# Where a transformer block's kernel copies and sums a set of combined weights

## The chip, the cores and the metric

The kernel runs on one core of a Trainium2 chip. The metric is the device time of one execution in microseconds; lower is better. The core has a matrix engine (TensorE, PE in the profile), a vector engine (VectorE, DVE), a scalar engine (ScalarE, ACT), GpSimd (POOL) and SyncE (SP). SP computes nothing here: it issues most of the transfers between the off-chip memory and the on-chip memory. ACT and POOL issue transfers too. Each engine works through its own list of instructions in order and waits on semaphores where an instruction needs another engine's or a transfer's result.

## The reference

One layer of a diffusion block, in fp32, for 1024 latent tokens and 256 context tokens of width 1024:

```python
h_x = _modulate(x, g_pre_mix[l], sh1, sc1)           # RMSNorm, gain, scale, shift
u_x, q_x, k_x, v_x = _project(h_x, w_in[l])
attn_x = _neighbourhood_attention(q_x, k_x, v_x, k_c, v_c, rpb[l])
mix_x = jnp.concatenate([_pool_mixer(u_x, pool_w[l], pool_scale[l]), attn_x], axis=-1) @ w_out[l]
x = x + gt1 * _rmsnorm(mix_x, g_post_mix[l])
y_x = _sq_relu_mlp(_modulate(x, g_pre_mlp[l], sh2, sc2), w_mlp_in[l], w_mlp_out[l])
x = x + gt2 * _rmsnorm(y_x, g_post_mlp[l])
```

The neighbourhood attention has 8 heads and adds a learned bias `rpb`, masked to a window, to the scores of the local keys. The MLP is relu(h @ w1) squared, times w2, with a hidden width of 4096.

## The kernel before

Every large product is done from operands split into a high and a low part (three matrix products for one), and most of the large products are one level of a seven-product scheme (Strassen's, in Winograd's form) over 2 x 2 blocks. That scheme needs sums and differences of the blocks of the weights. For the MLP's second product (`w2`), three such combinations are made ahead of time in off-chip memory, each in eight pages of 512 KB (g = 0 to 7): `t3` (block 1,1 plus block 0,1), `t1` (block 0,1 of `w2` plus block 0,0) and `t2` (block 1,1 plus `t1`). For each page there is one copy, `block_copied`, a transfer from `w2` to the page issued by SP (line 1329), and one sum, `block_summed`, a transfer that adds onto the page, issued by POOL (`add_to`, line 211). The 24 copies go in the order t3, t1, t2, and so do the 24 sums. The pages are first read in the second MLP product, from 815 us on (`t2`), 817 us on (`t3`) and 880 us on (`t1`).

The stages, in order of time: the normalised tokens and the pooling mixer's input, the context's keys, the values, then the *key products* (lines 1147 to 1176: 24 steps of twelve matrix products each, `step` 0 to 23, giving keys and queries), then *attention* (`for i in range(N)`, line 1447: 32 rounds, one for each of four pairs of heads and eight column tiles of 128 queries), the output projection, and the MLP: the *first product* goes over 16 pairs of hidden blocks (`block_pair(p)`, p = 0 to 15), the second over eight groups.

What sets the order: `with in_order(...)` ties every instruction of the listed engines to the one before it on the same engine in the block, as written; outside of it a planner orders each engine's list by its own estimate of when things are ready. The key products are in such a block for PE, POOL, ACT, DVE and SP (`pooling`), attention in another for PE, ACT, DVE and SP (`projected`) and one for POOL; pairs 1 to 14 of the MLP's first product are tied on PE and POOL.

Things to follow:
- `use(step)` splits the weights that were loaded four places ago and loads more (`load`, line 201) into a ring of four buffers, the tag `raw`. `mask_page()` at step 14 loads the mask (line 1057). `tables(0)` at step 20 loads the bias rows `U0w` (line 1069) into the same ring and has POOL subtract them from the mask into two pages `tab` (line 1077). `pool_mixed` at steps 21 and 22 splits the pooling mixer's output into pages `mix` of the same ring (lines 171 and 177).
- `key_parts` and `query_parts` split the keys and queries into high and low parts, `kP` and `qP`, which `scores(i)` reads (line 1223). `biased(i, e)` adds the tables to the scores (line 1243).
- In attention, round i issues two copies for i < 4 and one for 4 <= i < 16, after four ahead of the rounds, and `SUMS` lists the rounds that issue a sum. Five more sums go behind the output projection's rows.
- In the MLP's first product `summed_behind(c22)` (line 2024) lets ACT copy one column of a pair's result and POOL copy that again, so that the sum which POOL issues next comes no sooner than that result. Before the change, pairs 3 to 11 do so, once each.
- From pair 10 on, `ahead()` also sums up the row of the second gate, `accb`: POOL clears a page and loads a bias row (lines 238 and 239), and DVE adds eight weighted rows `wmb` to it (line 246).

Of the kernel before, what the change touches and what calls it, by code (L numbers as in the profile page):

```python
# [11 lines left out]
F32 = mybir.dt.float32  # L12
# [6 lines left out]
P = 128  # L19
# [84 lines left out]
def hybrid_block(ctx, tc, x, ctx_in, w_mod, mod_pages, w_u, b_mod, gp1, gp2, w_in, pool_w, rpb, w_out, w1, w2, vectors,  # L104
                 mask, edge, out):
    nc = tc.nc
    sub, mul, add = ALU.subtract, ALU.mult, ALU.add
# [6 lines left out]
    dram = ctx.enter_context(tc.tile_pool(name="dram", bufs=1, space=DRAM))  # L114
# [24 lines left out]
                last[i.engine] = i  # L139


    tiles = lambda a: a.rearrange("(m p) d -> m p d", p=P)
    xg, og = tiles(x), tiles(out)

# [62 lines left out]
        split(raw, hi, lo, factor)  # L207
        return hi, lo

    def add_to(to, more):  # L210
        nc.gpsimd.dma_start(to, more, accum_op=add)

    def pair(w, kk, c0, n):
        return w[2 * kk * P : (2 * kk + 2) * P, c0 : c0 + n].rearrange("(a p) f -> p a f", p=P)
# [79 lines left out]
    with tc.tile_pool(name="ps1", bufs=6, space=PSUM) as ps1, tc.tile_pool(name="tmp1", bufs=3) as tmp:  # L294

        def bank(name):
            if name[:2] == "pm" or name in ("pxt5", "pxb2", "pxb3", "pxb4", "pxb5", "pct2", "pct3"):
                return lasting(name)
            return ps1.tile([P, 512], F32, tag="mm", name=name)
# [74 lines left out]
        def put(copy, src, k, n):  # L374
            if xT[k] is None:
                xT[k] = page(f"xT{k}")
            copy(xT[k][:, n * P : n * P + src.shape[-1]], src)
# [628 lines left out]
        def fetch(n=1):  # L1006
            for get, _, i in islice(loads, n):
                get(i)

        def use(step):  # L1010
            for _, put, i in islice(uses, len(plan[step + 1]) if step + 1 < len(plan) else 0):
                put(i)
                fetch()
# [134 lines left out]
        with in_order(ET.PE, ET.Pool, ET.Activation, ET.DVE, ET.SP) as pooling:  # L1148
            banks = {of: [bank(f"p{of}{j}") for j in range(2)] for of in "KQ"}
            use(-1)  # L1150
            for step, (n, of, j) in enumerate([(n, of, j) for n, of in products for j in range(2)]):
                half_product(n, of, j, banks[of])
                use(step)
                if step in (5, 9, 17):
                    name = {5: "S1", 9: "S4", 17: "S3"}[step]
                    parts = token_operand(name, sraw[name])
                if step in (5, 7, 9, 11, 17, 19):
                    next(parts)
                    next(parts)
                if step in (7, 11):  # L1160
                    name = {7: "S4", 11: "S3"}[step]
                    sraw[name] = token_raw(name)
                if step == 14:
                    mask_page()
                if step == 20:
                    for _ in tables(0):
                        pass
                if step in (21, 22):
                    for g in range(2):
                        pool_mixed(2 * (step - 21) + g)  # L1170
                kept_product(n, of, j, banks[of][j])
                if step == 10:
                    kcs += [page(f"kc{n}", F32R) for n in "hl"]
                    split(kcp, *kcs)
                if step == 22:
                    key_parts(0, 0, True)


    w2v = w2.rearrange("(k i p) n -> i p k n", i=2, p=P)
    w2_block = lambda i, h, g: w2v[i][:, 2 * g : 2 * g + 2, h * 512 : (h + 1) * 512]  # L1180
    two_rows = lambda v: v.rearrange("p (a f) -> p a f", a=2)
    t1d, t2d = [[dram.tile([P, 3, 512], F32, tag=f"t{n}d_{g}", name=f"t{n}d_{g}")[:, :2] for g in range(8)] for n in (1, 2)]
    t3q = [dram.tile([P, 4, 1024], F32, tag=f"t3q{h}", name=f"t3q{h}") for h in range(2)]
    block_sums = []

    def block_summed():
        to, of, g = block_sums.pop(0)
        add_to(to(g), of(g))

    t1_page, t2_page, t3_page = t1d.__getitem__, t2d.__getitem__, lambda g: two_rows(t3q[g // 4][:, g % 4])  # L1190
    block_sums += [(to, of, g) for to, of in ((t3_page, lambda g: w2_block(0, 1, g)), (t1_page, lambda g: w2_block(0, 0, g)),
                                              (t2_page, t1_page)) for g in range(8)]

    with (
        tc.tile_pool(name="ps_s", bufs=2, space=PSUM) as ps_s,
# [126 lines left out]

        N = len(units)

        block_copies = [(to, i, g) for to, i in ((t3_page, 1), (t1_page, 0), (t2_page, 1)) for g in range(8)]

        def block_copied():
            to, i, g = block_copies.pop(0)
            nc.sync.dma_start(to(g), w2_block(i, 1, g))


        kks = (0, 1, 2, 3)
        raw_o, wo = {}, {}
        LOADS = (16, 20, 26, 28)
        SUMS = (9, 11, 12, 15, 15, 19, 23, 23, 27, 30)
        lows = []

        def high(src, hi, lo, pool=False):
# [73 lines left out]
        with in_order(ET.PE, ET.Activation, ET.DVE, ET.SP) as projected:  # L1412
# [8 lines left out]
            with tc.issue_after(pooling[ET.Pool]):  # L1421
                for k in range(4):
                    add_to(s3[k], s1a[k])
            for _ in range(4):
                block_copied()
            last_query("P7", 0)
            fillers = {0: [("P7", 1)], 1: [("P4", 0), ("P4", 1)]}
# [19 lines left out]
            for i in range(N):  # L1447
                if i in LOADS:
                    weight_load(0, kks[LOADS.index(i)])
                if i == N - 2:  # L1450
                    G1 = gate_page("a")
                if i > 3:
                    weighed(i - 4)
                if i == 0:
                    gain = mod_gain(gp1, att.tile([P, 256], F32, tag="gp", name="gpa"), nc.sync)
                    accs["sh"] = page("accsh2")
                    nc.sync.dma_start(accs["sh"], kept_row)
                if i == 2:
                    mod_gate("a", accs["a"], gain, rest_of_bank)
                if i in (5, 6):  # L1460
                    for k in (2 * i - 10, 2 * i - 9):
                        nc.sync.dma_start(sa2[k], s3[k])
                low()
                scores(i)
                biased(i, 0)
                if i < N - 1:
                    biased(i, 1)
                if 8 < i and i % 8 == 3:
                    right_added(i // 8 - 1)
                if 8 < i and i % 8 == 7:  # L1470
                    add_to(heads[i // 8 - 1][:, :512], sa2[i // 8 - 1])
                for f, *args in jobs.get(i, ()):
                    f(*args)
                for _ in range(2 if i < 4 else 1 if i < 16 else 0):
                    block_copied()
                for _ in range(SUMS.count(i)):
                    block_summed()
                if i == 2:
                    late_query = part_page("qP0_1", False)
                    qparts[0, 1] = late_query[:, :512], late_query[:, 512:]  # L1480
                    high_part(qT[0][1], qparts[0, 1][0])
                if i > 1:
                    turn(i - 2)
                    fifth_kept(i - 2)
                if i == 2:
                    turn_kept(0, 0, nc.scalar.copy)
                    column_sums("sc", accs["sc"], lambda name: pa[:, :256])
                if i == N - 1:
                    turn_kept(i - 2, 0, nc.scalar.copy)
                    turn_kept(i - 2, 1, nc.vector.tensor_copy)  # L1490
                    biased(i, 1)
                exps(i, 0)
                if i == 2:
                    column_sums("sh", accs["sh"], rest_of_bank)
                if 2 < i < N - 1:
                    turn_kept(i - 2, 0, nc.scalar.copy)
                exps(i, 1)
                if i == 0:
                    key_parts(2, 0, True, "lo")
                    key_parts(2, 1, True, "lo")  # L1500
                    query_parts(2, 0, False, "lo")
                if 1 < i < N - 1:
                    turn_kept(i - 2, 1, nc.vector.tensor_copy)
                if i == 2:
                    low_part(qT[0][1], *qparts[0, 1])
                for filler in fillers.get(i, ()):
                    last_query(*filler)
                if i > 2:
                    values(i - 3)
# [80 lines left out]
    with tc.tile_pool(name="ps2", bufs=6, space=PSUM) as ps2:  # L1590
# [6 lines left out]
      with ExitStack() as tmp2:  # L1597
# [58 lines left out]
        with tc.issue_after(projected[ET.DVE]), tc.issue_after(projected[ET.Activation]), in_order(ET.Activation, ET.DVE, ET.Pool) as added:  # L1656
# [20 lines left out]
            v = out_bank_sums("pov", "S3", wt3)  # L1677
# [343 lines left out]
            nc.vector.tensor_tensor(sb[:, 512:], r12, sa[:, 512:], sub)  # L2021
            defer(keep, "S4", p, sb[:, 512:])

        def summed_behind(src):
            pace = sm("pace" + str(len(block_sums)) + "_", 2)
            nc.scalar.copy(pace[:, :1], src[:, :1])
            nc.gpsimd.tensor_copy(pace[:, 1:], pace[:, :1])
            block_summed()

        spilled = []  # L2030

# [4 lines left out]
        def block_pair(p, ahead, final=False):  # L2036
# [15 lines left out]
            c22 = part(f"c22_{p}")  # L2052
            nc.scalar.copy(c22, z)  # L2053
            ahead()
            v = bank(f"phv{p}")
# [2 lines left out]
            nc.vector.tensor_tensor(c22, c22, u2, add)  # L2058
            squared(c22, c22)
            defer(keep, "A22", p, c22)  # L2060
            if 2 < p and block_sums:
                summed_behind(c22)
            if p >= EARLY:
                r11 = second_sum(p, x)
            if not final:
# [177 lines left out]
        with tc.issue_after(first[ET.PE]), in_order(ET.PE, ET.Activation, ET.DVE, ET.SP, ET.Pool):  # L2243
# [139 lines left out]
            y, z, u2, c22 = four("pyy"), None, s1, None  # L2383
            less = lambda to, a, b: nc.vector.tensor_tensor(to, a, b, sub)
            for name, g in items[items.index(("P6", 0)) : items.index(("P4", 0))]:
# [8 lines left out]
                else:  # L2394
                    if g == NG - 1:
                        c22 = whole("N")
# [12 lines left out]
            v = four("pyv")  # L2409
# [79 lines left out]
```

## Time and profile before

| what | value |
|---|---|
| median of 3 runs | 1020.87 us (1020.83 to 1021.02) |
| the profiled execution | 1019.65 us, span 1017.9 us |
| PE busy | 1004.5 us (99% of the span) |
| DVE, ACT, POOL busy | 784.2, 572.3, 204.8 us |
| granted TensorE clock | 0.999 |
| transfers | 256.33 MB, mean 252 GB/s |
| first matrix product of the key products' first step | 146.19 us |
| PE's first scores of attention | 214.28 us |
| the 24 copies | issued from 34.7 us (four of them) and from 217.8 to 251.1 us |
| the 24 sums | issued from 250.3 to 636.5 us |

The span goes from the first to the last instruction of the profiled execution; its own time, with what lies around the span, is 1.75 us more. In the order of time a row gives the start, the duration, the engine, the line, the operation, what it writes and reads, and in brackets the idle time of the engine before it and what ended it. SPq is the issuing of transfers by SP. A row of a stretch gives its length, then the busy time of PE, PE's weight loads, DVE, ACT and POOL, the granted clock, the busy share of the 16 DMA engines and the GB/s that they moved. "DMA to landing" is the time from the issue of a transfer to its arrival. A row of waits gives the total in us, how many, and the longest.

### The profile page before, as it was taken

To read this page: it belongs to the slowest core of one execution; us is meant where nothing else is said; L and a number is where in the kernel's file an instruction comes from. 1 tells how busy PE (TensorE), PEld (TensorE's weight loads), DVE (VectorE), ACT (ScalarE), POOL (GpSimd) and SP (SyncE) were. 2 spreads that over 40 slices of the span, in tenths; PEclk is the share of its full clock that TensorE was granted. 3 is DMA by queue.
4 is the path that set the end of the run, shared out by engine and by line. 5 is a ranking of instruction groups with operands and counts; after the bars stand their busy time and mean duration, and the time that the engine had idled before them with its cause. 6 is when DMAs were issued, how large, how long until landed. Compare 5 with 4: busy or idle time off the path is not lost.

```text
span 1017.9 us, 17064 instructions
## 1 busy us (share of the span) xinstructions
PE 1004.5 (99%) x6298; PEld 843.3 (83%) x6298; DVE 784.2 (77%) x1216; ACT 572.3 (56%) x997; POOL 204.8 (20%) x287
## 2 busy tenths in 40 slices
PE   8999999999999999999999999999999999999997
PEld 5788888878998888888888887888888888888886
DVE  5588767967885689879988877764797878787795
ACT  6672254348886746786555544555556455544451
POOL 4111200166985232410010110000000000012021
PEclk9999999999999999999999999999999999999999
DMA  9999798669989979986789877634997696699944
GB/s 365 390 290 322 256 259 301 209 158 324 236 182 251 229 203 269 302 211 199 258 234 279 253 230 230 200 141 181 335 356 229 206 369 211 203 276 295 303 166 164
DMA packets 148036, 256.33 MB, mean 252 GB/s; under 512 B 10545, under 2 KB 76977, under 8 KB 147953
## 3 DMA queue, kind: packets, MB, share of 16 engines
q1 hardware_dynamic: 113200, 185.82, 53.7%
q0 software_dynamic: 17616, 38.45, 20.0%
q10 hardware_dynamic: 17136, 30.97, 8.2%
q8 instruction: 49, 0.80, 0.3%
q14 instruction: 35, 0.28, 0.1%
HBM read 201.71 MB, written 77.61 MB: 274 GB/s over the span
## 4 chain that ended last, share of the span: by engine, by line
PE 85%; DMA 6%; DVE 5%; issue 2%; ACT 1%; POOL 0%; SPq 0%; ACTq 0%; DVEq 0%
PE pu L476 4%; PE pa L1310 4%; PE S L1223 3%; PE pyx L221 3%; PE pyx L222 3%; PE pyx L223 3%; PE phx L221 2%; PE phx L222 2%; PE phx L223 2%; DMA wa_1w<-in_w 2%; PE phz L221 2%; PE phv L221 2%; PE phz L223 2%; PE phv L223 2%; PE phv L222 2%
## 5 line engine op out<-in xcount | busy, mean ns | idle before, releaser
L1930 ACT ACTIVATE c<-c 128x512 f32<-128x512 f32 x48 | 30.3, 631 | 60.5 <-DVE c L2058 36.7
L1254 ACT ACTIVATE sp<-sp,nm 128x640 f32<-128x640 f32 (+1 forms) x64 | 51.4, 804 | 6.1 <-DVE ri L1258 4.9
L1243 DVE CUSTOM_DVE_ANT_0 sp<-S,tab 128x640 f32<-128x640 f32 (+1 forms) x56 | 44.6, 796 | 13.3 <-PE pz L1276 10.4
L175 DVE TENSOR_TENSOR wpS<-S,wpS 128x512 fp32r<-128x512 f32 x64 | 43.5, 687 | 9.3 <-ACT wpS L169 9.3
L221 PE MATMUL phx<-thB,wpA 128*128 128x512 f32 x128 | 50.2, 392 | 0.0
L169 ACT CAST wpS<-S 128x512 fp32r<-128x512 f32 x64 | 38.5, 614 | 20.3 <-DVE S L1903 7.8
L222 PE MATMUL phx<-tlB,wpA 128*128 128x512 f32 x128 | 49.8, 389 | 0.0
L223 PE MATMUL phx<-thB,wpA 128*128 128x512 f32 x128 | 49.8, 389 | 0.0
L2138 POOL COPY pace_t<-t 128x1 f32<-128x1 f32 x8 | 4.3, 538 | 204.0 <-DMA t<-t1d 204.0
L1931 ACT ACTIVATE c<-c 128x512 f32<-128x512 f32 x48 | 30.3, 631 | 15.2 <-DVE sa L2015 12.3
L221 PEld LDWEIGHTS phx<-thB,wpA 128*128 128x128 f32 x128 | 24.0, 188 | 5.5 <-ACT s L1983 0.4
L223 PEld LDWEIGHTS phx<-thB,wpA 128*128 128x128 f32 x128 | 24.0, 188 | 5.0
L222 PEld LDWEIGHTS phx<-tlB,wpA 128*128 128x128 f32 x128 | 24.0, 188 | 4.9
L221 PE MATMUL phv<-thT,wpA 128*128 128x512 f32 x64 | 25.3, 395 | 2.0 <-DVE c L2057 2.0
L1310 PE MATMUL pa<-pt,v 128*64 128x128 f32 x352 | 25.8, 279 | 0.0
L221 PE MATMUL phz<-thB,wpS 128*128 128x512 f32 x64 | 25.3, 395 | 0.5 <-ACT c L2053 0.5
L222 PE MATMUL phv<-tlT,wpA 128*128 128x512 f32 x64 | 24.9, 390 | 0.0
L223 PE MATMUL phz<-thB,wpS 128*128 128x512 f32 x64 | 24.9, 390 | 0.0
L223 PE MATMUL phv<-thT,wpA 128*128 128x512 f32 x64 | 24.9, 389 | 0.0
L222 PE MATMUL phz<-tlB,wpS 128*128 128x512 f32 x64 | 24.9, 389 | 0.0
L221 PE MATMUL phy<-thT,wpS 128*128 128x512 f32 x64 | 24.9, 389 | 0.0
L222 PE MATMUL phy<-tlT,wpS 128*128 128x512 f32 x64 | 24.9, 389 | 0.0
(1219 smaller groups left out, 3678.4 us busy)
## 6 DMA issues: line engine op xcount, KB each, us to landing
hrA<-hdA SPq DMA_DIRECT2D x24, 512.0 KB, 6.9
wm<-in_mod_pages SPq DMA_DIRECT2D x16, 512.0 KB, 9.4
wa_0w<-in_w SPq DMA_DIRECT2D x16, 512.0 KB, 5.5
wa_1w<-in_w SPq DMA_DIRECT2D x16, 512.0 KB, 5.0
hdA<-c ACTq DMA_DIRECT2D x32, 256.0 KB, 3.8
hdS<-sa ACTq DMA_DIRECT2D x32, 256.0 KB, 5.3
hqS<-sb ACTq DMA_DIRECT2D x32, 256.0 KB, 5.4
b<-in_w SPq DMA_DIRECT2D x16, 512.0 KB, 7.1
```

The source lines that it names most:

```text
L169: nc.scalar.copy(hi, src)
L175: nc.vector.tensor_tensor(lo, src, hi.bitcast(F32), sub)
L221: nc.tensor.matmul(ps, ahi, bhi, start=first, stop=False, skip_group_check=more)
L222: nc.tensor.matmul(ps, ahi, blo, start=False, stop=False, skip_group_check=more)
L223: nc.tensor.matmul(ps, alo, bhi, start=False, stop=last, skip_group_check=more)
L476: nc.tensor.matmul(pus[b][j], wk(wgt, k, low, j * P, P), r, start=(k == 0 and n == 0), stop=(k == KT - 1 and n == 2))
L1223: nc.tensor.matmul(S[e][:, c0 : c0 + k[0].shape[1]], q[n_q][hs, cols], k[n_k][hs], start=(n_q + n_k == 0), stop=(n_q == 1))
L1243: nc.vector.tensor_tensor_reduce(out=to, in0=s, in1=bt, scale=1.0, scalar=BIG, op0=add, op1=ALU.min, accum_out=nm)
L1254: nc.scalar.activation(sp, sp, AF.Exp, bias=least[i, e], scale=-1.0, accum_out=sums[i][:, e : e + 1])
L1310: nc.tensor.matmul(pa[e * HD : (e + 1) * HD, cols], v[:, f : f + HD], turns[i][:, e, c] if c < 4 else fifths[i][:, :, (e + 1) * HD : (e + ...
L1930: nc.scalar.activation(r, src, AF.Relu)
L1931: nc.scalar.activation(r, r, AF.Square)
```

## The change

The definitions of the pages, copies and sums move up, unchanged. Twelve of the 24 copies are issued within the key products, one in each of the steps 12 to 23, right after `use(step)`; three instead of four ahead of the rounds of attention; none in rounds 0 to 6; and one in each round from 7 on until all are out (rounds 7 to 15). Two sums in attention move by a round (15 to 16, 23 to 22). The last nine sums go behind pairs 10 to 14 of the MLP's first product, two at a time and the last alone, instead of one behind each of the pairs 3 to 11.

```diff
@@ key products
                 half_product(n, of, j, banks[of])
                 use(step)
+                if 11 < step:
+                    block_copied()
                 if step in (5, 9, 17):
@@ attention
-        SUMS = (9, 11, 12, 15, 15, 19, 23, 23, 27, 30)
+        SUMS = (9, 11, 12, 15, 16, 19, 22, 23, 27, 30)
@@
-            for _ in range(4):
+            for _ in range(3):
                 block_copied()
             last_query("P7", 0)
@@
-                for _ in range(2 if i < 4 else 1 if i < 16 else 0):
+                if 6 < i and block_copies:
                     block_copied()
                 for _ in range(SUMS.count(i)):
                     block_summed()
@@ MLP, first product
-        def summed_behind(src):
+        def summed_behind(src, n):
             pace = sm("pace" + str(len(block_sums)) + "_", 2)
             nc.scalar.copy(pace[:, :1], src[:, :1])
             nc.gpsimd.tensor_copy(pace[:, 1:], pace[:, :1])
-            block_summed()
+            for _ in range(n):
+                block_summed()
@@
-            if 2 < p and block_sums:
-                summed_behind(c22)
+            if 9 < p and block_sums:
+                summed_behind(c22, min(2, len(block_sums)))
```

More of the change, by code (lines that the diff above doesn't have):

```diff
@@ L139, in in_order, with add_to, block_summed, block_copied @@
                 last[i.engine] = i
+    def add_to(to, more):
+        nc.gpsimd.dma_start(to, more, accum_op=add)
+    w2v = w2.rearrange("(k i p) n -> i p k n", i=2, p=P)
+    w2_block = lambda i, h, g: w2v[i][:, 2 * g : 2 * g + 2, h * 512 : (h + 1) * 512]
+    two_rows = lambda v: v.rearrange("p (a f) -> p a f", a=2)
+    t1d, t2d = [[dram.tile([P, 3, 512], F32, tag=f"t{n}d_{g}", name=f"t{n}d_{g}")[:, :2] for g in range(8)] for n in (1, 2)]
+    t3q = [dram.tile([P, 4, 1024], F32, tag=f"t3q{h}", name=f"t3q{h}") for h in range(2)]
+    block_sums = []
+    def block_summed():
+        to, of, g = block_sums.pop(0)
+        add_to(to(g), of(g))
+    t1_page, t2_page, t3_page = t1d.__getitem__, t2d.__getitem__, lambda g: two_rows(t3q[g // 4][:, g % 4])
+    block_sums += [(to, of, g) for to, of in ((t3_page, lambda g: w2_block(0, 1, g)), (t1_page, lambda g: w2_block(0, 0, g)),
+                                              (t2_page, t1_page)) for g in range(8)]
+    block_copies = [(to, i, g) for to, i in ((t3_page, 1), (t1_page, 0), (t2_page, 1)) for g in range(8)]
+    def block_copied():
+        to, i, g = block_copies.pop(0)
+        nc.sync.dma_start(to(g), w2_block(i, 1, g))
     tiles = lambda a: a.rearrange("(m p) d -> m p d", p=P)
@@ L208, in high_low @@
         return hi, lo
-    def add_to(to, more):
-        nc.gpsimd.dma_start(to, more, accum_op=add)
     def pair(w, kk, c0, n):
@@ L1176, in hybrid_block @@
                     key_parts(0, 0, True)
[L1179 to L1192, printed above, removed]
     with (
@@ L1323, in hybrid_block @@
         N = len(units)
[L1325 to L1329, printed above, removed]
         kks = (0, 1, 2, 3)
```

## The prediction

> **What bounds the kernel now.** I read the page first, then the busy time by stretch, then the order of time on SP, POOL, ACT and DVE around the two places that the diff touches.
>
> ```profile
> PE 1004.5 (99%) x6298; PEld 843.3 (83%) x6298; DVE 784.2 (77%) x1216; ACT 572.3 (56%) x997; POOL 204.8 (20%) x287
> ```
>
> TensorE is busy 99% of the span. The change takes no matmul away, so it can win only PE's idle time, 1017.9 - 1004.5 = 13.4 us, most of it at the start and the end, which the diff doesn't touch. It can lose without limit wherever a moved transfer makes PE wait. So I look for what each moved transfer stands in front of.
>
> **Part 1: twelve copies within the key products (steps 12 to 23).** Each is one transfer of 512 KB from DRAM to DRAM, issued by SP with nothing to wait for. The block is in order on SP, so each stays behind its step's weight loads and ahead of whatever SP issues next. In the trace SP's order at that place is this:
>
> ```profile
> 186.02 0.32 SPq L201 DMA_DIRECT2D wKT4w<-wKT  x1
> 187.82 0.32 SPq L201 DMA_DIRECT2D wQT3w<-wQT  x1
> 189.55 0.32 SPq L201 DMA_DIRECT2D wQT4w<-wQT  x1
> 189.97 0.38 SPq L1057 DMA_DIRECT2D msk<-in_mask  x1
> 191.41 1.23 SPq L1069 DMA_DIRECT2D U0w<-in_rpb  x2
> ```
>
> Loads wKT4 and wQT3 belong to steps 12 and 13, wQT4 and the mask to step 14, the bias rows U0w to step 20. SP runs ahead of the other engines: nothing but the queue's order and a free buffer held U0w back until 191.41. After the change copy 1 stands behind wKT4, copy 2 behind wQT3, copy 3 behind wQT4, and copies 4 to 9 between the mask and U0w. Nine copies are ahead of U0w. Do later transfers of a queue wait for earlier ones? The burst of copies in attention's first rounds shows it:
>
> ```profile
> 217.76 4.90 SPq L1329 DMA_DIRECT2D t3q<-in_w  x4
> 222.71 4.65 SPq L1329 DMA_DIRECT2D t1d<-in_w  x5
> ```
>
> ```profile
> L1329 SPq DMA_DIRECT2D t3q<-in_w x1: 1716/1716/1716, 217.8 to 217.8; - x1
> ...
> DMA to landing us min/median/max: 9.0/9.0/9.0
> ```
>
> ```profile
> L1329 SPq DMA_DIRECT2D t1d<-in_w x2: 552/584/616, 224.9 to 226.8; - x2
> ...
> DMA to landing us min/median/max: 13.3/13.5/13.7
> ```
>
> ```profile
> 225.00:240.00 15.00, 14.87 (x261) 12.87 (x262) 12.68 (x34) 12.26 (x33) 7.92 (x20) 1.00 1.05 353
> ```
>
> The first copy lands at 217.8 + 9.0 = 226.8, the ninth at 226.8 + 13.7 = 240.5: eight landings in 13.7 us, 1.71 us each, and the wait grows along the burst, as in a line. The stretch 225 to 240 moves 353 GB/s with the DMA engines full, so 524,288 bytes take 1.49 us. I price a copy at 1.49, nine at 13.4 us; the high end is 1.71, 15.4 us. The low end is what SP needs to issue them where four went out in a row:
>
> ```profile
> 34.74 4.41 SPq L1329 DMA_DIRECT2D t3q<-in_w  x4
> ```
>
> That is 1.10 us each, 9.9 us. The engines have no room to hide it: they are full while U0w's predecessors drain.
>
> ```profile
> 190.00:195.00 5.00, 5.00 (x24) 4.14 (x23) 4.51 (x7) 2.09 (x3) 0.00 (x0) 1.00 0.99 339
> 195.00:200.00 5.00, 5.00 (x24) 4.14 (x23) 4.22 (x6) 2.19 (x3) 0.31 (x1) 1.00 0.14 37
> ```
>
> ```profile
> L1069 SPq DMA_DIRECT2D U0w<-in_rpb x2: 585/588/591, 191.4 to 192.1; - x2
> ...
> DMA to landing us min/median/max: 5.3/5.5/5.6
> ```
>
> U0w lands at 192.1 + 5.5 = 197.6 now, and at 211.0 after (207.5 to 213.0). Who waits for it: POOL builds the bias tables from it, and ACT's next split waits for POOL, because the page that it writes is U0w's old buffer.
>
> ```profile
> L1077 POOL TENSOR_TENSOR tab<-msk,U0w x12: 439/446/1425, 200.4 to 206.8; 128x128 f32<-128x128 f32 x12
> ```
>
> ```profile
> 200.41 6.85 POOL L1077 TENSOR_TENSOR tab<-msk,U0w 128x128 f32<-128x128 f32 x12
> ```
>
> ```profile
> 207.30 1.15 ACT L171 ACTIVATE mix<-y 128x512 fp32r<-128x512 f32 x2 [4.63 <-POOL tab L1077]
> ```
>
> ACT, which is in order, now waits 4.63 us there, and behind it stand the key and query parts that PE's first scores read:
>
> ```profile
> 207.96 1.29 DVE L177 SCALAR_TENSOR_TENSOR mix<-y,mix 128x512 fp32r<-128x512 f32 x2 [1.05 <-ACT mix L171]
> ...
> 211.67 0.69 DVE L1140 TENSOR_TENSOR kT<-pK,kT 128x512 f32<-128x512 f32 x1 [1.21 <-PE pK L223]
> 212.27 0.68 DVE L175 TENSOR_TENSOR qP<-q,qP 128x512 fp32r<-128x512 f32 x1
> ```
>
> ```profile
> 214.62 0.28 PE L1223 MATMUL S<-kch,qP 64*128 64x256 f32 x2
> ```
>
> From the release at 207.26, DVE needs until 212.27 + 0.68 - 1.21 (a wait for PE that would be over by then) = 211.74 for the query's low part, and PE reads it at 214.62: a slack of 2.9 us. After the change POOL starts at 211.0. Its twelve operations take 12 x 0.446 = 5.35 us if none is slowed, because DVE will stand idle then, and 6.85 us as they ran. I take 5.35: the release comes at 216.35, 9.1 us late, and PE stalls 9.1 - 2.9 = **6.2 us** before its first scores. Ends: copies of 1.10 us give a release at 212.85 and a stall of 2.7; copies of 1.71 us with 6.85 us of tables give 219.85 and 9.7. PE's work is in order and there is 99% of it, so nothing gives this back.
>
> The range of the tables' time has a rule beside it. The Trainium skill (SBUF — State Buffer, section SBUF: two separate sides) says that GpSimd and a VectorE operation with two SBUF inputs lock each other out of one port pair. By it the tables take 5.35 us while DVE waits and the stall is 6.2; without it they take 6.85 and the stall is 7.7. The spread of one operation, 446 to 1425 ns beside DVE's splits, agrees. The same skill's page DMA: Bandwidth & Descriptors (section Anatomy of one DMA) has data move at 436 GB/s; an estimate by that is 1.20 us for a copy, 10.8 for nine, and a stall of 3.6; the measured 353 GB/s decides.
>
> Other loads that copies pass: wQT3 has one ahead of it, wQT4 two, 3.0 us, and the mask three; the mask is read together with U0w, which is later. wQT4, issued at 189.55, is read at
>
> ```profile
> 200.56 1.06 ACT L171 ACTIVATE wQT4h<-wQT4w 128x1024 fp32r<-128x1024 f32 x1 [1.19 <-PE pQ L222]
> ```
>
> and ACT's idle time before it ended with PE, not with the load: 11 us for a load of the kind that took 5.5 and 3.0 more; free. Copies 10 to 12 follow U0w and delay only the first gate's gain and a kept row, used from round 2 on. Of the three copies left ahead of the rounds the order of time suggests that they take the place of the four at 34.74, which no row shows as late for anybody; 0, between -0.3 and +0.3.
>
> **Part 2: none in rounds 0 to 6, one a round from 7.** Copies leave a stretch where PE never waits on a DMA, and nine go where eight were issued in a burst. I put 0 on it. The two sums moved by a round are free: no reader before the second MLP product.
>
> **Part 3: last nine sums, two at a time, behind pairs 10 to 14 instead of one behind each of pairs 3 to 11.** Seven sums leave pairs 3 to 9, and five come to 10 to 14, net of those there.
>
> ```profile
> 530.00:535.00 5.00, 4.70 (x21) 3.59 (x20) 4.75 (x9) 2.33 (x5) 0.00 (x0) 1.00 0.98 154
> 545.00:550.00 5.00, 4.80 (x21) 3.66 (x20) 4.74 (x9) 2.77 (x5) 0.00 (x0) 1.00 0.86 264
> 630.00:635.00 5.00, 3.03 (x14) 2.15 (x13) 4.19 (x6) 1.38 (x3) 0.00 (x0) 1.00 0.36 105
> ```
>
> ```profile
> PE phv L221 <- DVE c L2057: 2.0, 1, 2.0
> ```
>
> ```profile
> 594.22 0.81 POOL L211 DMA_DIRECT2D t2d<-t1d  x1
> 594.75 1.25 POOL L238 MEMSET accb<- 128x1024 f32 x1
> 596.29 0.53 POOL L239 DMA_DIRECT2D accb<-in_b_mod  x1 [0.30 <-POOL accb L238]
> ```
>
> ```profile
> 602.37 1.28 DVE L246 SCALAR_TENSOR_TENSOR accb<-wmb_0w,sx,accb 128x1024 f32<-128x1024 f32 x1 [2.94 <-DMA accb<-in_b_mod]
> ```
>
> PE idles 0.30 + 0.20 + 1.97 = 2.5 us in these stretches. The last is DVE coming late, and DVE lost 2.94 us to the second gate's row (its add to accb waits for the row's load), whose clearing and load POOL issued behind pair 9's sum at 594.22, in order. With no sum in pairs 3 to 9 that issue is free to go early. Against it stand one more sum at pair 10 and one at 11:
>
> ```profile
> q0 software_dynamic: 17616, 38.45, 20.0%
> ```
>
> 20% of 1017.9 us for 38.45 MB is 2.78 us for 0.524 MB. If both push the same loads, the cost is 5.56 - 2.94 = +2.6 us; if neither does, the gain is 2.5. I take a gain of **1.5**, nearer to the measured 2.94 us that surely goes.
>
> **Sum.** Against the profiled execution's 1019.65 us (span 1017.9): 1019.65 + 6.2 - 1.5 = 1024.4. That execution is 1.22 under the median 1020.87, so the forecast is **1025.6 us**.
>
> **Rivals.** *No stall.* Where U0w lands before 204.8, the slack of 2.9 covers it; that needs copies under 7.2 / 9 = 0.80 us each, or a queue that lets U0w pass. Then only part 3 counts: 1019.4, with the whole of the idle time 1018.4. For it: the DMA engines are 14% busy from 195 to 200, so the copies find room there, if U0w got through first. Against it: the growing landings above. *Stall and crowded pairs.* Two sums at a time hold up the loads of pairs 11 and 12: 1020.87 + 6.2 + 2.6 = 1029.7. For it: the loads there already come from DVE's late releases. *The sums change nothing*, because something else holds the gate row back: 1027.1, inside the first case's range.
>
> **How the numbers follow.** The stall with some gain has 0.70 (own range 1022.5 to 1028), no stall 0.16, stall and crowding 0.14. 0.2%, 2 us, is about what a measurement of this kernel can tell from no change. Half of the second case is faster, 0.08; its other half and the shortest stalls of the first, 0.13, are within; slower is 0.79. The range 1020.5 to 1029.5 leaves out the fast end of the second case and the slow end of the third.
>
> **What would show it.** Right: U0w issued behind nine copies and landing about 13 us later against the key products; ACT's wait for POOL's tables near 14 us; a PE gap of about 6 us before the first scores; the row accb issued before pair 9's end and no 2 us gap at pair 11. Wrong: U0w landing within 7 us of now, or a second wait of PE in pairs 11 to 14.

## The result, and the profile after

The changed kernel takes 1031.33 us (median; 1029.85 to 1032.32) where the kernel before takes 1020.85: a ratio of 1.0104, interval 1.0087 to 1.0122. It is slower, as forecast, but by 10.5 us and not by 4.7; 1031.33 lies above the forecast's range. The profiled execution took 1032.32 us with a span of 1030.5, against 1019.65 and 1017.9 before. One execution of experiment 6 took 1676.53 us at a granted clock of 0.556 and stands outside every median and ratio below.

The page's row of busy time:

```profile
PE 1009.3 (98%) x6298; PEld 847.0 (82%) x6298; DVE 784.2 (76%) x1216; ACT 573.3 (56%) x993; POOL 201.4 (20%) x283
```

The span grew by 12.6 us. TensorE's idle time grew by 7.8 (from 13.4 to 21.2), and its busy time by 4.8, for the same 6298 matmuls. That second number is the first thing to see: a matmul got slower somewhere. What TensorE waited for:

```profile
PE phv L242 <- DVE c L2059: 5.9, 3, 2.7
PE S L1231 <- DVE kT L1161: 5.4, 1, 5.4
```

Before, the first row read 2.0, once, and the second was not there. So the idle time is +5.4 before the first scores and +3.9 in the pairs' waits, or +3.4 with the two short idles of 0.2 and 0.3 that went; the rest is -1.0, a wait for POOL about round 7 of attention that is gone, -0.6 at the start and +0.6 in a product ahead of attention. The last two needn't come from the change: the profiles of experiments 2, 7 and 9, which leave the start as it was, run ahead there by as much, and the wait ahead of attention isn't in experiments 1 and 3. Now the place before the scores, SP first:

```profile
186.56 0.32 SPq L224 DMA_DIRECT2D wKT4w<-wKT  x1
186.94 0.57 SPq L163 DMA_DIRECT2D t3q<-in_w  x1
...
191.17 0.62 SPq L1078 DMA_DIRECT2D msk<-in_mask  x1
191.84 5.30 SPq L163 DMA_DIRECT2D t3q<-in_w  x5
197.41 0.55 SPq L163 DMA_DIRECT2D t1d<-in_w  x1
199.21 1.21 SPq L1090 DMA_DIRECT2D U0w<-in_rpb  x2
```

Nine copies stand ahead of `U0w`, which is issued at 199.21 instead of 191.41 and lands 11.4 us later instead of 5.5. POOL, ACT and DVE follow in turn, each with the idle time before it in brackets:

```profile
210.74 4.94 POOL L1098 TENSOR_TENSOR tab<-msk,U0w 128x128 f32<-128x128 f32 x12 [10.00 <-DMA U0w<-in_rpb]
```

```profile
215.71 0.63 ACT L194 ACTIVATE mix<-y 128x512 fp32r<-128x512 f32 x1 [11.87 <-DMA gpa<-in_gp]
```

```profile
216.37 1.76 DVE L200 SCALAR_TENSOR_TENSOR mix<-y,mix 128x512 fp32r<-128x512 f32 x1 [7.88 <-ACT mix L194]
...
219.26 0.68 DVE L1161 TENSOR_TENSOR kT<-pK,kT 128x512 f32<-128x512 f32 x1
219.86 0.67 DVE L198 TENSOR_TENSOR qP<-q,qP 128x512 fp32r<-128x512 f32 x1
```

ACT's row names a load as the releaser; its start at 215.71, at the end of the tables (210.74 + 4.94 = 215.68), says that it is the tables. TensorE's rows after that show where matmuls got slower:

```profile
220.08 0.58 PE L1231 MATMUL S<-kch,qP 64*128 64x256 f32 x2 [5.44 <-DVE kT L1161]
...
222.76 0.63 PE L244 MATMUL pqv<-S3h,wQT3l 128*128 128x512 f32 x1
223.19 0.63 PE L242 MATMUL pqv<-S3h,wQT3h 128*128 128x512 f32 x1
```

```profile
220.00:222.00 2.00, 1.92 (x13) 1.72 (x14) 1.89 (x4) 0.00 (x0) 1.66 (x4) 0.50 1.04 172
222.00:224.00 2.00, 2.00 (x5) 1.56 (x6) 1.15 (x4) 0.00 (x0) 0.00 (x0) 0.50 1.12 192
```

The column behind the five busy times is the granted clock: 0.50. Equal matmuls start 0.43 us apart (222.76, 223.19), 0.23 apart at full clock. The same happens once more, at pair 11:

```profile
639.01 0.80 PE L242 MATMUL phv<-thT,wpA 128*128 128x512 f32 x1 [2.75 <-DVE c L2059]
...
643.45 0.63 PE L243 MATMUL phv<-tlT,wpA 128*128 128x512 f32 x1
643.87 0.63 PE L244 MATMUL phv<-thT,wpA 128*128 128x512 f32 x1
```

Each stretch of half clock is 6.83 us long. It begins within an idle time of TensorE, of 5.44 and 2.75 us, and goes on behind it. Together they make the 4.8 us of longer busy time, within some 0.3: from the first scores (214.28 before, 220.08 now) to a product 24 matmuls on (217.61, 225.74) the kernel falls another 2.3 us behind, and in the same way another 2.8 at pair 11. In the pairs, POOL and then DVE read:

```profile
592.27 0.55 POOL L260 DMA_DIRECT2D accb<-in_b_mod  x1 [0.30 <-POOL accb L259]
...
617.22 1.18 POOL L143 DMA_DIRECT2D t1d<-in_w  x1
617.95 1.34 POOL L143 DMA_DIRECT2D t2d<-t1d  x1
```

```profile
630.22 1.28 DVE L267 SCALAR_TENSOR_TENSOR accb<-wmb_5w,sx,accb 128x1024 f32<-128x1024 f32 x1 [6.26 <-DMA wmb_5w<-in_w_mod]
```

The second gate's row `accb` does go out early, at 592 instead of 596, while the work around it runs some 6 us later. But the two sums behind pair 10 stand ahead of the gate's load `wmb_5w`: it lands in 10.3 us instead of 6.3, and DVE waits for it 6.26 us instead of 2.2. At pairs 12 and 13, where TensorE waits 0.79 and 2.35 us, there is no gate load left. There the pair's own weights are late: `wa_1w` lands in 9.1 and 11.4 us instead of 5.7 and 4.2, and DVE waits 6.17 and 5.47 us for it.

### The profile page after: what moved, and what is told of

Read it like the earlier page. It is cut to its first block, busy times and chain, and to the rows that moved or that the text cites. A ratio compares the mean times of both kernels' runs of the same rounds, so it can differ in the third digit from the quotient of the medians.

```text
span 1030.5 us, 17066 instructions
## 1 busy us (share of the span) xinstructions
PE 1009.3 (98%) x6298; PEld 847.0 (82%) x6298; DVE 784.2 (76%) x1216; ACT 573.3 (56%) x993; POOL 201.4 (20%) x283
## 4 chain that ended last, share of the span: by engine, by line
PE 76%; DMA 12%; DVE 7%; issue 3%; ACT 1%; SPq 0%; DVEq 0%; ACTq 0%; POOL 0%; POOLq 0%
PE pu L497 4%; PE pa L1318 3%; PE S L1231 3%; PE pyx L242 3%; PE pyx L243 3%; PE pyx L244 3%; PE phv L242 3%; PE phv L243 2%; PE phv L244 2%; PE phx L242 2%; PE phz L242 2%; PE phx L243 2%; PE phx L244 2%; PE phz L243 2%; PE phz L244 2%
## 5 line engine op out<-in xcount | busy, mean ns | idle before, releaser
L198 DVE TENSOR_TENSOR wpS<-S,wpS 128x512 fp32r<-128x512 f32 x64 | 43.4, 687 | 10.3 <-ACT wpS L192 10.3
L242 PE MATMUL phv<-thT,wpA 128*128 128x512 f32 x64 | 26.4, 412 | 5.9 <-DVE c L2059 5.9
L244 PE MATMUL phv<-thT,wpA 128*128 128x512 f32 x64 | 25.9, 404 | 0.0
```

Source lines behind the costliest of these rows:

```text
L198: nc.vector.tensor_tensor(lo, src, hi.bitcast(F32), sub)
L242: nc.tensor.matmul(ps, ahi, bhi, start=first, stop=False, skip_group_check=more)
L244: nc.tensor.matmul(ps, alo, bhi, start=False, stop=last, skip_group_check=more)
```

## The experiments

Theory: (1) the copies stand in line ahead of `U0w`; (2) two sums at a time hold up the loads of the pairs that follow, 10 to 13; (3) an idle time of TensorE of some 2.7 us or more brings a stretch of half clock behind it. The rivals: the copies cost something else than the line; part 3 gains, and the copies are all of the loss; the half clock has a cause of its own. Ratios are to the kernel before, run beside each of them.

**1. The twelve copies behind the tables.** 

```diff
-                if 11 < step:
-                    block_copied()
...
                 if step == 20:
                     for _ in tables(0):
                         pass
+                if 19 < step:
+                    for _ in range(3):
+                        block_copied()
```

> The changed kernel, but its twelve copies within the key products are issued after the bias rows U0w (three in each of the steps 20 to 23) instead of from step 12 on. Queue theory (nine copies ahead of U0w in SP's queue hold back the tables, ACT behind them, and PE; the long idle time then halves TensorE's clock): U0w lands near 198 us as before the change, ACT waits about 4.6 us for the tables, PE does not wait before its first scores, and one of the two stretches of half clock is gone; the pairs' waits stay. That is 1031.3 - 5.4 (wait) - 2.4 (half clock) = about 1023.5 us. Rival (the copies hurt by their traffic wherever they stand in the key products): PE still waits over 3 us before the scores, 1027 us or more.

Measured: 1024.32 us, 1.0046 (1.0032 to 1.006). `U0w` is issued at 192.1 and the tables are built from 199.65, as before; TensorE doesn't wait before the scores. Moving the copies behind one load takes the ratio from 1.0104 to 1.0046, some 6 of the 10.5 us, and the line is the reason. What is left is in the pairs: three waits of 6.1 us in all, and one stretch of half clock of 3.41 us.

**2. The sums alone:** the kernel before with part 3.

```diff
-            if 2 < p and block_sums:
-                summed_behind(c22)
+            if 9 < p and block_sums:
+                summed_behind(c22, min(2, len(block_sums)))
```

> The kernel before, with only the third part of the change: the last nine sums behind pairs 10 to 14, two at a time. Crowding theory (two sums at a time hold up the loads of the pairs that follow): PE waits 2 to 3 us at each of the pairs 11 and 13 and just under 1 at 12, one stretch of half clock behind pair 11; 1020.9 + 3.4 + 2.4 = about 1026.7 us. Rival (the pairs' waits in the changed kernel come from the later phase that the first stall gives everything, not from the sums): at most the 2.5 us of waits of before, and with the gate's row early less, 1018.5 to 1021 us.

Measured: 1025.68 us, 1.0058 (1.0043 to 1.0072). Part 3 by itself costs 0.58%, some 6 us. The waits, and the stretch behind the longer one:

```profile
PE phv L221 <- DVE c L2058: 5.2, 2, 3.6
```

```profile
650.00:655.00 5.00, 1.93 (x5) 1.54 (x6) 4.75 (x8) 0.72 (x2) 0.00 (x0) 0.70 0.00 0
655.00:660.00 5.00, 5.00 (x16) 3.92 (x15) 2.73 (x5) 4.28 (x9) 1.82 (x3) 0.62 0.62 121
```

TensorE's waits grow from 2.0 to 5.2 us, and the clock is at half for 6.83 us from 652.0.

**3. The copies alone:** the changed kernel with one sum behind each of pairs 3 to 11, as before.

```diff
-            if 9 < p and block_sums:
-                summed_behind(c22, min(2, len(block_sums)))
+            if 2 < p and block_sums:
+                summed_behind(c22, 1)
```

> The changed kernel with the last nine sums put back, one behind each of the pairs 3 to 11. Queue theory with crowding theory: the wait of 5.4 us before the first scores and its half clock of 2.4 us stay, the pairs wait as before the change (2.5 us in all, no half clock there): 1020.9 + 5.4 + 2.4 - 1.0 (a wait in rounds 6 and 7 that the changed kernel does not have) = about 1027.7 us. Rival (the pairs' waits come from the later phase): the waits of 2.75, 0.8 and 2.35 us stay, 1031 us.

Measured: 1027.21 us, 1.0071 (1.0058 to 1.0084). In the profile TensorE waits 6.0 us before the scores, with 6.83 us of half clock behind it, and 2.7 at pair 11, with 3.41 us of half clock behind that, which was not expected. The two parts cost 0.7% and 0.6% alone and 1.04% together.

**4. Six copies ahead instead of nine:** in steps 12 to 17, the other six behind the tables.

```diff
-                if 11 < step:
+                if 11 < step < 18:
                     block_copied()
...
+                if step in (20, 21):
+                    for _ in range(3):
+                        block_copied()
```

> The changed kernel with six copies, of steps 12 to 17, ahead of the bias rows' load and the other six behind the tables. Theory (a line of 1.49 us a copy): the rows land 8.9 us later than in the kernel before, POOL's release comes 4.6 us late against a slack of 2.9, TensorE stalls about 1.7 us before the first scores, too short for a half clock there: 1024.3 (all twelve behind the tables) + 1.7 = 1026.0, 1.005 of before. Rival (cost is all or nothing, since the engines take some copies for free): no stall, 1024.3. Rival (any stall starts the half clock): 1028.4.

Measured: 1026.42 us, 1.0066 (1.0046 to 1.0085). POOL's tables, and TensorE's first scores:

```profile
205.10 5.17 POOL L1098 TENSOR_TENSOR tab<-msk,U0w 128x128 f32<-128x128 f32 x12 [5.29 <-DMA U0w<-in_rpb]
```

```profile
214.21 0.38 PE L1234 MATMUL S<-kch,qP 64*128 64x256 f32 x2 [0.49 <-DVE kT L1161]
...
215.19 0.38 PE L1234 MATMUL S<-kch,qP 64*128 64x256 f32 x2 [0.49 <-DVE qP L198]
```

Nine copies moved `U0w` from 197.6 to 210.7, six to 205.1: 1.46 and 1.25 us a copy. The stall is 1.0 us where 1.7 was expected, and no half clock follows. The dose fits the line and the slack. The median is 2.1 above that of experiment 1, twice the stall, and the intervals overlap. In the profiled executions the rest is in the pairs: waits of 7.3 us for 6.1, and 6.83 us of half clock for 3.41.

**5. Work put into the wait, first try:** 22 matmuls behind the last query product, into a page `pz` of PSUM (the memory that takes the matrix products) that was thought to be free.

```diff
             last_query("P7", 0)
+            for _ in range(22):
+                nc.tensor.matmul(pz, weights["T4", "Q"][0][:, :P], rows_of["A22"][0][0], start=True, stop=True)
```

> The changed kernel with 22 extra matrix products of 128x512, about 5.0 us of PE's time at full clock, put between the last product of the key products' kind and the first scores; their result goes to a bank that is written over later, so they only keep PE busy while it would wait. Clock theory (the clock is halved because PE stood idle for more than 5 us, and the half clock costs another 2.4 us): PE's clock stays whole from 214 to 226 us, PE's wait there is under 1 us, and the time is about 1029 us. Rival (the clock falls for another reason, or the idle time alone is the price): 1031.3 us or more.

Measured: 1036.72 us, 1.0167 (1.0154 to 1.018). It says nothing of the clock, since the added work waited too:

```profile
PE pz L1429 <- DVE kT L1161: 5.7, 1, 5.7
```

`pz` isn't free. By the wait that ended both, it lies like the scores in a bank of PSUM that held a key product, and DVE's last read of that product (`kT`, at 219.26 in the changed kernel) must come first. So the scores wait for the bank as well as for the query's low part. Both come from the same chain behind ACT's split, 0.6 us apart.

**6. Second try:** the query's last product done three times in its own bank, 24 more matmuls ahead of the wait.

```diff
+            for _ in range(2):
+                half_product("P7", "Q", 0, last_queries)
             last_query("P7", 0)
```

> The changed kernel with the query's last product of its first half done three times into its own bank: 24 more matmuls of 0.2265 us, 5.44 us of work, where TensorE idles 5.44 us before its first scores. Theory (the half clock after the first scores follows from TensorE's idle time ahead of them): the granted clock stays near 1.0 from 214 to 226, the stretch of doubled matmul spacing is gone there, and 2.4 us come back: 1028.9 us, 1.008 of the time before. Rival (the half clock comes from something else at that place, or idle time is not what counts): no change, 1031.3. Second rival: the extra work ends after DVE's chain and delays the scores; up to 1 us slower.

Measured: 1029.78 us, 1.0107 (1.0086 to 1.0128): not told apart from the changed kernel's time, as the first rival said. But the place itself changed as the theory says. TensorE waits 0.3 us before the scores, and the clock stays whole:

```profile
220.00:222.00 2.00, 2.00 (x16) 1.60 (x15) 2.00 (x5) 0.00 (x0) 1.12 (x3) 1.00 1.11 191
222.00:224.00 2.00, 2.00 (x12) 1.45 (x12) 1.25 (x4) 1.59 (x3) 0.00 (x0) 1.00 1.10 173
```

The first product that reads `px` starts at 239.6 instead of 242.2, 2.6 us earlier. The first scores already start 0.5 us earlier (219.54 for 220.08), so 2.1 us came back behind them; 2.4 were expected. In the profiled execution 1.9 of the 2.6 are lost again about 270, around a wait of 1.49 us for which the profile names no releaser, and the pairs' waits come to 6.9 us instead of 5.9. In five executions the mean granted clock is 0.996, against 0.993 for the changed kernel's four. One stretch of 6.83 us at half clock is 0.0033 of the span, so this is about what one stretch less would make; which one is gone only the profile shows. That this stretch of half clock follows from the idle time ahead of it is shown. Its full price came back up to 270 and not in the total; where the rest went in the executions without a profile stays open.

**7. One sum moved:** the kernel before, with pair 9's sum behind pair 12.

```diff
-            if 2 < p and block_sums:
+            if 2 < p and p != 9 and block_sums:
```

> The kernel before with one edit: the sum behind pair 9 goes behind pair 12, one at a time as all others. Theory (POOL's sum at pair 9 holds back the second gate's row, nothing else makes the 2 us gap at pair 11): the row's load goes out about 592, the gap of 1.97 us goes and the sum at pair 12 costs nothing: 1018.9, 0.998 of before. Rival (a gap of the loads takes its place, as where two sums stand behind pair 10): 1020.9 or more.

Measured: **1017.69 us, 0.9975** (0.9963 to 0.9987). The row of the second gate goes out ten us earlier, and the wait at pair 11 is gone; one of 1.7 us is left a pair later, at 649.

```profile
586.16 0.53 POOL L239 DMA_DIRECT2D accb<-in_b_mod  x1 [0.30 <-POOL accb L238]
```

```profile
PE phv L221 <- DVE c L2057: 1.7, 1, 1.7
```

So a gain of the size that was promised for part 3 is there, with one sum out of the way and not nine put in pairs. That the row is the cause isn't shown: in the profile TensorE idles 13.5 us (1016.8 - 1003.3) as it did before (13.4), since the 1.7 us, and 0.8 us more about 540, stand in place of the 2.0.

**8. That sum moved, and the copies behind the tables.** The edits of 1 and 7 in the changed kernel.

> The changed kernel with its twelve copies behind the tables, and one sum behind each of pairs 3 to 8 and 10 to 12. Both theories together: no stall before the first scores, no crowded pairs, the 1 us wait in attention's second round and 0.6 us at the start gone: about 1017.5, 0.997 of before. Rival (copies behind the tables cost something of their own): 1020.9 or more.

Measured: 1017.21 us, 0.9973 (0.9961 to 0.9984). Faster than before, but not told apart from experiment 7. Its profile has one wait that no other has, 1.48 us from 345.7 on in the output projection; whether the copies bring it is open.

**9 and 10. All sums before pair 9:** two behind each of pairs 3 to 5, one behind 6 to 8; in the kernel before, and in the changed kernel with the copies behind the tables.

```diff
             if 2 < p and block_sums:
                 summed_behind(c22)
+                if p < 6:
+                    block_summed()
```

> The kernel before with its last nine sums two at a time behind pairs 3 to 5 and one behind pairs 6 to 8, so none stands beside the second gate's loads of pairs 10 to 12. Theory (a sum costs where the gate's loads share the queues, and two at a time is no harm by itself): the wait of 1.7 us that is left at pair 12 where pair 9 alone was skipped goes too: 1017.7 - 1.7 = 1016.0, 0.9955 of before. Rival (two sums at a time hold up loads wherever they stand): waits of TensorE in pairs 4 to 6, 1017.7 or more.

> The same sums (two behind pairs 3 to 5, one behind 6 to 8) in the changed kernel with its twelve copies behind the tables. Theory: 0.5 us under the kernel with these sums alone, as the copies behind the tables gave where pair 9 was skipped (1017.2 against 1017.7): 1015.5, 0.995 of before. Rival (the copies' new place brings a wait of its own after attention): 1016.0 or more.

Measured: 1023.67 us, 1.0039 (1.0026 to 1.0053), and 1019.4, 1.0001 (0.9992 to 1.0009); 1016.0 and 1015.5 were expected. My theory that two at a time do no harm away from the gate's loads fell. Pairs 10 to 13 have no wait at all, as I expected, but the first kernel's waits now read:

```profile
PE phz L221 <- ACT c L2053: 3.8, 2, 3.3
```

The 3.3 end at 536.2. Behind two sums, issued at 511.3 and 512.1, the pair's weights `wa_1w`, issued at 516.4, land in 11.2 us instead of 7.4 in the kernel before, and DVE waits 6.4 us for them instead of 3.2; the waits of the second kernel are of the same kind, 6.1 in all. Two sums behind one another hold up a pair's own weights here too, as at pairs 12 and 13 of the changed kernel.

**11 and 12. One sum behind each of pairs 0 to 8,** in the kernel before, and in the changed kernel with the copies behind the tables.

```diff
-            if 2 < p and block_sums:
+            if block_sums:
```

> The kernel before with its last nine sums one behind each of pairs 0 to 8 instead of 3 to 11. Theory (a sum is free when it stands alone and no gate load stands beside it): no wait in pairs 10 to 13, as with two sums behind pairs 3 to 5, and none in pairs 3 to 5 either: 1016.0, 0.9955 of before. Rival (pairs 0 to 5 have no room for a sum, since their kept rows are read back there): a wait in pairs 1 to 5, 1017.7 or more.

> The same sums, one behind each of pairs 0 to 8, in the changed kernel with its twelve copies behind the tables. Theory: 0.5 us under the kernel with these sums alone: 1015.5, 0.995 of before. Rival: the wait in pairs 1 to 5, 1017.2 or more.

Measured: 1021.53 us, 1.0019 (1.001 to 1.0028), and **1016.0 us, 0.9963** (0.9949 to 0.9977), the fastest of all. In neither does TensorE wait in pairs 10 to 13, nor more than 0.3 us in any pair; in the profile of the second it idles 10.5 us in all (1014.2 - 1003.7), 2.9 less than before. The first loses in attention instead:

```profile
247.06 1.21 POOL L211 DMA_DIRECT2D t1d<-in_w  x1 [1.79 <-DMA t1d<-in_w]
247.81 0.76 POOL L1260 COPY rb<-ri 128x128 f32<-128x128 f32 x1
```

```profile
PE pa L1276 <- POOL rb L1260: 3.8, 1, 3.8
```

In both kernels the first of the nine sums is now issued in attention about round 7, not in the first product, so that these two also differ there from what their edit says. In the kernel with the burst of copies, POOL waits there for the copy that it adds to; `rb` stands behind it, TensorE waits 3.8 us, and the clock is at 0.60 from 250 to 255. With the copies behind the tables that copy, issued at 235.8, has landed, POOL issues the sum at 243.65 with next to no wait, and TensorE waits 1.2 us for `rb`. Here copies ahead of attention pay.

## Why the prediction was wrong

**Part 1, right in mechanism, near in size.** `U0w` was to land at 211.0 and POOL started at 210.74: the 1.49 us a copy was right. The tables took 4.94 us instead of 5.35, with no slow operation among them while DVE stood still. The Trainium skill's rule of the shared port (SBUF — State Buffer, section SBUF: two separate sides) held with that. By the 436 GB/s of the Trainium skill (DMA: Bandwidth & Descriptors, section Anatomy of one DMA), which stands there for transfers that GpSimd issues, the row would have landed at 208.4, an estimate that is 2.3 us too soon. The release came at 215.68 for 216.35, the stall was 5.4 us for 6.2. That the scores wait for a PSUM bank, not only for the query's low part, the prediction had not seen; it changes the slack by less than 1 us.

**The step that is missing: what a stall does to the clock.** The prediction ends at "TensorE stalls 6.2 us" and counts a stall as its own length. Half clock followed for 6.83 us, which cost another 2.3 here, and 2.8 at pair 11. The sum needed a term of 4.8 us, by TensorE's busy time. With it the working would have come to 1030.4, near the measured time by luck, since part 3 would still have been 4.9 off. The profile before had nothing to warn of it: its clock is 0.999 and not 1 for a half clock from 1016.5 us on, where TensorE has had no work since 1011.9. Its executions run beside the experiments do differ with the clock, 1020.6 us in the mean of 21 with a clock of 0.996 or 0.997, 1019.3 in 25 with 0.999 or 1.0. The Trainium skill (TensorE: Matmul & The Clock Gate, section Part 1: The HAM clock gate (the "warmup" mystery)) has the clock go to half after one idle window of about 3.4 us, in windows that run freely. The lengths agree: 3.41 and 6.83 us are one window and two. The idle time doesn't: of the 3.41 us ahead of the stretch at pair 11 TensorE idles 2.0 (636.26 to 638.23), and that was enough.

**Part 2, near.** It was put at 0. No reader missed a copy in rounds 0 to 6, and TensorE's wait of 1.0 us for POOL about round 7 went; the profiles of experiments 1, 3, 8 and 10, which move the copies, don't have it either.

**Part 3, wrong in sign.** "I take a gain of 1.5" is the step that failed. The early row, worth 2.94 us of DVE's wait, came as described, and experiment 7, which lets the row go early with no second sum anywhere, is 0.25% faster, 2.5 us. But the cost of "one more sum at pair 10 and one at 11" was bounded at 5.56 - 2.94 = +2.6, as so many bytes more, and pairs 12 to 14 were left out: not five but seven sums come to pairs 10 to 14, nine less the two that stood there. TensorE's waits grew by 3.4, most of that at pairs 12 and 13. A load that comes behind two sums lands 4 us late or more (10.3 for 6.3, 11.4 for 4.2), and DVE waits for it; with the half clock behind them part 3 costs some 4 us (1031.33 against experiment 3's 1027.21) to 6 (experiment 2). The rival "stall and crowded pairs", put at 0.14, is what happened. Its 1029.7 lies close by luck: it too has no half clock, and with 4.8 us more it would come to 1034.5.

**The ledger:** stall 5.4, pairs' waits 3.4, half clock 4.8, and -1.0 - 0.6 + 0.6 for round 7, the start and the product ahead of attention: 12.6 us, the growth of the span between the two profiled executions; the medians are 10.5 apart. The forecast had 6.2 - 1.5 = 4.7. The 7.9 between them are 4.8 of half clock, 4.9 of part 3's waits, -0.8 of the stall and -1.0 of what else went.

## What to carry to other kernels

A transfer with nothing to wait for still takes its turn: before moving one up in a queue, look for the load that is issued next behind it, and whose buffer waits on that load; behind `tables(0)` the same twelve copies cost nothing that the times show. When TensorE is at 99%, a new idle time of 2 us or more is to be priced at its length, and beside it at its length plus a half clock behind it, 1.7 us (half of 3.41) to 2.8 here; which of the two comes hangs on where the idle time falls, as below. And these background transfers did least harm one at a time: two behind one another cost more than two apart in both places tried, pairs 3 to 5 and pairs 10 to 13.

## What the hardware showed that I had not expected

- Half clock keeps to windows of 3.41 us, and theory (3), that the length of an idle time decides, doesn't hold. In each profile the starts and ends of its stretches lie whole multiples of 3.413 us apart (in the changed kernel 218.4, 225.2, 638.2 and 645.1: 2, 121 and 2 windows). From 10 us on and ahead of TensorE's last product there are fourteen stretches in the profiles of all runs. In the window just ahead of each, TensorE idles 1.89 us or more. Of the windows at full clock with no stretch behind them one has 1.94 us idle, the others 1.77 or less. So 1.93 us were enough in experiment 5, where they fell into one window, and 2.80 and 3.31 us brought nothing in experiment 10, where each fell across two windows, at most 1.94 us in one:

```profile
664.00:667.60 3.60, 1.67 (x8) 1.06 (x7) 3.57 (x7) 0.09 (x1) 0.00 (x0) 1.00 0.02 5
667.70:671.00 3.30, 3.30 (x10) 2.52 (x9) 0.88 (x2) 3.27 (x8) 1.50 (x3) 0.50 0.26 101
```

```profile
530.00:540.00 10.00, 7.20 (x32) 5.64 (x31) 8.10 (x14) 5.00 (x10) 1.13 (x2) 1.00 0.95 209
546.00:556.00 10.00, 6.69 (x30) 5.22 (x29) 9.29 (x16) 5.00 (x10) 0.00 (x0) 1.00 0.98 271
```

- A stretch of half clock lasted two windows, 6.83 us, in the seven cases where TensorE was still idle as it began, and one, 3.41 us, in the seven where TensorE was at work again. Equal matmuls then start 0.43 us apart for 0.23. How idle times and windows fall in the executions without a profile can't be seen; the clock of the kernel before went down to 0.996 in some.
- A load of 512 KB took 10.3 us instead of 6.3 to land behind one more sum of 512 KB, 4 us for bytes that the prediction priced at 2.78.
- A releaser named in a wait can be wrong: ACT's 11.87 us are put down to a load, where POOL's tables ended in the very moment it went on.
